# Turned transposes in the set-up of a state-space branch, and two idle products on TensorE

## The chip, the cores and the metric

The kernel runs on one core of a Trainium2 chip, as one launch. The metric is the time of the launch on the device in microseconds (us). The core's engines are TensorE (PE in the profile; its weight loads are the row PEld), VectorE (DVE), ScalarE (ACT), GpSimd (POOL) and SyncE (SP). Each works off its own queue of instructions in order and waits on semaphores for what the others make. SP's and POOL's queues also hold the instructions that start DMA transfers: one that waits holds up all behind it on that queue.

## What is computed

One layer of an encoder over 512 tokens of width 1024, with 256 fixed memory tokens, in fp32:

```
n = rms_norm(h);  proj = n @ w_in            # columns: xa 512, zu 1024, zv 1024, gate_a 1024, gate_b 1024
ya = s5_branch(xa)                           # two diagonal state-space scans (forward, backward), 32 groups of 16
     y = d*u + scan_fwd(u) + scan_bwd(u);  y = gelu(y);  ya = y * sigmoid(y @ w_glu)
yb = sgu_branch(zu, zv)                      # gating by 128x128 position matrices
h = h + (gate_a*(ya @ w_proj_a) + gate_b*(yb @ w_proj_b)) @ w_out
q = rms_norm(h) @ w_q;  k, v = memn @ w_k, memn @ w_v    # memn = rms_norm(mem); 4 heads of 256
h = h + softmax(q k^T / 16) v @ w_o
h = h + (silu(n @ w_gate) * (n @ w_up)) @ w_down;  out = rms_norm(h)
```

## The kernel before, in words

**Products.** Every fp32 operand is split into a high and a low half in a reduced format: ScalarE casts the high half (L85), VectorE subtracts it for the low one (L86). A product is three matmuls, high by high, high by low, low by high (`mm3`, L358). `feat` makes two banks of 128 channels x 512 tokens at a time (tiles `pf`), `tokm` makes banks of 128 tokens x 512 channels (`pt`). For w_proj_b, w_q and the feed-forward part the kernel multiplies 2x2 blocks with seven products instead of eight (`product`, L1110; 128x256 each), on sums of blocks that are made ahead. The intermediate banks of w_proj_b are `bx`, `bq`, and `qv` for a copy of a bank by ScalarE that later products go on adding to (`seed`, L1123). `gated` (L1173) multiplies a bank with a gate in `part`; the last one is `gated(1, 1, T0, minus(bq, u1))`, where `u1` lies in the tile `zf[0]`.

**Weights** come through a plan: three raw buffers filled by DMAs on SP's queue (L137, L224), split two blocks ahead of their use into three buffers of halves.

**The S5 branch as a side program.** `s5_program` is a Python generator: set-up, kernels of octets 0 and 1, inputs, scan, outputs, with the kernels of octets 2 and 3 between the outputs. The main program calls `tick(us)` after each block of products; a tick adds credit (0.8 of the block's time) and runs the generator until the credit is used up. `yield 1.1` costs 1.1 of it; `yield None` ends the tick and sets the credit to nothing. `later(n, fn)` puts a function off by n steps of 5.2 us.

- Set-up (L625 on): the input and output matrices are loaded as rows (`brow`, `crow`) and turned on TensorE, 8 transposes (L657) and 4 transposes (L664) to an auxiliary PSUM bank, each bank copied by ScalarE to `raw_b` (L658) or `raw_c` (L665).
- Kernels (`pk`, L814-817) are matrices of 8x8 steps within a chunk, stored to DRAM and loaded back. Inputs: `pw` transposes (L864), `pz` products (L871). The scan (L890-901) is a chain of small VectorE operations on `zh`, one step for each of 64 chunks.
- Outputs, for each octet of groups: four copies of states `ss` on ScalarE (L916, L917), 24 products pairwise `py` (L922 to L924), gelu to `y` (L929), and eight stores `yd` to DRAM (L932), by turns on SP and POOL.

**Merging.** `finish_side` runs the rest of the side program. Then four loads `ygt` (SP, L1222) bring the S5 outputs back in another layout; they are split to `yg` and multiplied by w_glu; the sigmoid (L1229), the product `glu` (L1231) and a split give `ya`, which goes through w_proj_a. The rows of gains `g_mem` and `g_x` are loaded on SP (L471); they use the two buffers of the tag "gain", one of which is `zf[0]`'s.

**Order.** The framework builds the program with a scheduler that simulates a timeline (`schedule_with_timeline_sim=True`) and chooses the order on every engine; `tc.keep_in_program_order` fixes single instructions (`in_order`), among them the loads of `g_mem` and `g_x` and the idle products. An idle product is a matmul of 128x512 to an auxiliary bank that nobody reads:

```python
    def idle_product(x, y):
        in_order(nc.tensor.matmul(aux("idle"), x[:, 0, 0:P], y[:, 4, :], start=True, stop=True))
```

There are two in the kernel already, at the second query product and in the feed-forward part. Auxiliary banks are three; the banks of the main products are five.

**Keys.** After w_out, `feat` makes the keys (`w_k`, four pairs of tiles of 128x256), then `tokm` the values (`w_v`), then follow the queries (`qx`, `qq`).

Of the kernel before, what the change touches and what calls it, by code (L numbers as in the profile page):

```python
# [9 lines left out]
F32 = mybir.dt.float32  # L10
# [7 lines left out]
P = 128  # L18
# [8 lines left out]
G = 32  # L27
C = 16
# [13 lines left out]
NO = 4  # L42
# [10 lines left out]
def hybrid_layer_kernel(  # L53
# [8 lines left out]
    nc = tc.nc  # L62
# [14 lines left out]
    def bank(name):  # L77
        return pm.tile([P, 512], F32, tag="mm", name=name)

    def aux(name, shape=(P, 512)):  # L80
        return pa.tile(list(shape), F32, tag="aux", name=name)
# [248 lines left out]
    def next_w(*key):  # L330
        i = used_w[0]
        used_w[0] += 1
        assert len(plan[i][0]) == len(key) and plan[i][0][1:] == key[1:] and plan[i][0][0] is key[0]
        for j in range(i, min(i + FAR + 1, len(plan))):
            begin(j, i)
            if j - 1 >= len(tiles) and j - 1 <= i + SPLITS:
                split_w(j - 1)
        for j in range(len(tiles), min(i + SPLITS + 1, len(plan))):
            split_w(j)
        tile_, tiles[i] = tiles[i], None  # L340
        return tile_
# [20 lines left out]
    def feat(w, c0, act, nk, evac, n=T, kpt=4, parts=1, ps=None, part=None):  # L362


        if part is not None:
            for kb in range(0, nk, kpt):
                feat_block(ps, (kb,) + next_w(w, kb, kpt, c0, 256), act, nk, kpt, part[0], not part[1])
                tick(2.6)
            if part[1]:
                for j in range(2):  # L370
                    evac(c0 // P + j, j, ps[j])
            return
        ps = ps or [bank("pf0"), bank("pf1")]
        ws = []
        for kb in range(0, nk, kpt):
            ws.append((kb,) + next_w(w, kb, kpt, c0, 256))
            if parts == 1:
                feat_block(ps, ws.pop(), act, nk, kpt, slice(0, n))
                tick(5.2 * n / T)
        for i in range(parts if parts > 1 else 0):  # L380
            for x in ws:
                feat_block(ps, x, act, nk, kpt, slice(i * n // parts, (i + 1) * n // parts))
            tick(5.2 * len(ws) / parts)
        for j in range(2):
            evac(c0 // P + j, j, ps[j][:, :n])

    def feat_block(ps, x, act, nk, kpt, tsl, fresh=True):

        kb, hi, lo = x
        for j in range(2):  # L390
            cs = slice(j * P, (j + 1) * P)
            for k in range(kpt):
                kk = kb + k
                mm3(ps[j][:, tsl], (hi[:, k, cs], lo[:, k, cs]), (act[0][:, kk, tsl], act[1][:, kk, tsl]),
                    kk == 0 and fresh, kk == nk - 1, not fresh)
# [47 lines left out]
    def later(n, fn):  # L443

        side["later"].append((side["now"] + n, fn))
# [7 lines left out]
    def tick(us=5.2):  # L453

        side["now"] += us / 5.2
        run_due()
        side["credit"] = min(side["credit"] + us * side["rate"], us)
        while side["credit"] > 0.0 and side["gen"] is not None:
            try:
                used = next(side["gen"])  # L460
            except StopIteration:
                side["gen"] = None
                return
            if used is None:
                side["credit"] = 0.0
                return
            side["credit"] -= used
# [8 lines left out]
    ident = cp.tile([P, P], F32, name="ident")  # L476
# [61 lines left out]
    def slot(tag, shape, dt, name, place=NEAR):  # L538
        n = math.prod(shape[1:])
        t = sp.tile([P, KD * T + ROOM[tag]], dt, tag=tag, name=name)[:, place[tag]:place[tag] + n]  # L540
        return t.rearrange("p (a b c) -> p a b c", a=shape[1], b=shape[2]) if len(shape) == 4 else (
            t.rearrange("p (a b) -> p a b", a=shape[1]))

    def token_slot(name, place=NEAR):
        return tuple(slot(tag, (P, KD, T), F32R, name, place) for tag in "BC")
# [3 lines left out]
    s5p = s5.enter_context(tc.tile_pool(name="s5", bufs=1))  # L549
# [70 lines left out]
    def s5_setup():  # L620
        A_ = nc.scalar
# [3 lines left out]
        def small():  # L625
            used[0] += 1
            return slab[:, used[0] - 1, :]
# [6 lines left out]
        for i, src in enumerate((s5_lam_re, s5_lam_im)):  # L634
            nc.sync.dma_start(lrows[:, i], src[0].rearrange("d g p -> g d p"))
            ps = aux("plam", (P, G))
# [11 lines left out]
        crow = s5p.tile([P, 2, C // 4, 2, 64], F32, tag="tt", name="crow")  # L648
# [2 lines left out]
                nc.sync.dma_start(crow[:, i, :, d, :], src[0, d].rearrange("g (a b) p -> (g a) b p", a=4))  # L651
        bb = s5p.tile([P, 2, G, C], F32, name="raw_b")
        rows = brow.rearrange("g d p c -> g (d p) c")
        for n in range(2):
            ps = aux("pbc", (P, C // 2, 2 * G))
            for k in range(C // 2):
                nc.tensor.transpose(ps[:, k, :], rows[:, :, 8 * n + k], ident[:2 * G, :2 * G])  # L657
            A_.copy(bb.rearrange("p i g c -> p c (i g)")[:, 8 * n:8 * n + 8, :], ps)  # L658
            yield None
        cc = s5p.tile([P, 2, G, C], F32, name="raw_c")  # L660
        for i in range(2):
            ps = aux("pbc", (P, C // 4, P))
            for k in range(C // 4):
                nc.tensor.transpose(ps[:, k, :], crow[:, i, k].rearrange("q d p -> q (d p)"), ident)  # L664
            A_.copy(cc[:, i].rearrange("p g (a b) -> p b (g a)", a=4), ps)  # L665
            yield 0.1
        br, bi, cr, ci = bb[:, 0], bb[:, 1], cc[:, 0], cc[:, 1]
        st["c"] = (cr, ci)

# [1 line left out]
        stp, a, rho, th, n, sn, hs, cs = (small() for _ in range(8))  # L671
# [103 lines left out]
    def lc(t, g):  # L775
        return t[:, g].rearrange("p a b -> p (a b)")
# [127 lines left out]
    def s5_outputs(o):  # L904
        gs = slice(o * GO, (o + 1) * GO)
        while ("oct", o) not in st:
            yield None
        e_re, e_im, tt = st["oct", o]
        zh, u = st["zh"], st["u"]
        ss = s5p.tile([P, 2, GO, NCH], F32, tag="wt", name="ss", bufs=2)  # L910
        ss = (ss[:, 0], ss[:, 1])
        for i, s in enumerate(ss):
            zv = zh[:, :, i, gs].rearrange("p n g -> p g n")
            nc.gpsimd.memset(s[lo_, :, 0:1], 0.0)
            nc.gpsimd.memset(s[hi_, :, NCH - 1:NCH], 0.0)
            nc.scalar.copy(s[lo_, :, 1:NCH], zv[lo_, :, 0:NCH - 1])  # L916
            nc.scalar.copy(s[hi_, :, 0:NCH - 1], zv[hi_, :, 0:NCH - 1][:, :, ::-1])  # L917

        def mix_():
            ps = aux("py", (P, GO, NCH))  # L920
            for g in range(GO):
                nc.tensor.matmul(ps[:, g, :], tt[:, g, :], u[:, o * GO + g, :], start=True, stop=False)  # L922
                nc.tensor.matmul(ps[:, g, :], lc(e_re, g), ss[0][:, g, :], start=False, stop=False)
                nc.tensor.matmul(ps[:, g, :], lc(e_im, g), ss[1][:, g, :], start=False, stop=True)  # L924
            later(1, lambda: emit(ps))

        def emit(ps):
            y = s5p.tile([P, GO, NCH], F32, tag="y", name="y")
            nc.scalar.activation(y, ps, AF.Gelu_apprx_tanh)  # L929
            ydo = yd[o].rearrange("(g c) l n -> l c g n", c=C)  # L930
            for l in range(Q):
                (nc.sync, nc.gpsimd)[l % 2].dma_start(ydo[l], y[C * l:C * l + C])  # L932

        later(0.5, mix_)
        yield 0.1

# [123 lines left out]
    for h in range(H):  # L1060
        ps = bank("psv")
# [7 lines left out]
    yb_hi = slot("E", (P, KD, T), F32R, "yb_hi", AWAY)  # L1069
    yb_lo = slot("D", (P, KD, T), F32R, "yb_lo", AWAY)  # L1070
# [43 lines left out]
    def idle_product(x, y):  # L1114

        in_order(nc.tensor.matmul(aux("idle"), x[:, 0, 0:P], y[:, 4, :], start=True, stop=True))

    def unit_bank(name):
        return bank(name).rearrange("p (j t) -> p j t", j=2)
# [45 lines left out]
    for q, ts in ((5, T1), (6, T0)):  # L1165
        for i in range(2):
            k = slice(2 * i, 2 * i + 2)
# [98 lines left out]
    hn_hi, hn_lo = token_slot("hn", AWAY)  # L1266
# [53 lines left out]
    def v_evac(half):  # L1320
        def f(t, ps):
            if not vts:
                vt = ap_.tile([P, 2, NM, D], F32R, tag="vt", name="vt", bufs=1)
                vts.extend((vt[:, 0], vt[:, 1]))
            vt_hi, vt_lo = vts
            cs = slice(half * 512, half * 512 + 512)
            split(vt_hi[:, t, cs], vt_lo[:, t, cs], ps)
        return f
# [20 lines left out]
    later(2, token_sums)  # L1349
    for c0 in range(0, D, 256):  # L1350
        feat(w_k, c0, mn, KD, k_evac, n=M)
    for half in range(2):
        tokm(w_v, half * 512, mn, KD, v_evac(half), ntok=NM)

# [132 lines left out]
    for t0 in (0, 2):  # L1487
        ps = {t: bank(f"pt{t - t0}") for t in (t0, t0 + 1)}
# [77 lines left out]
    ps = [bank("pf0"), bank("pf1")]  # L1566
# [67 lines left out]
    for i, u in enumerate(UNITS):  # L1634
        final = i == len(UNITS) - 1
        x, v = begun
        q = unit_bank("pq")
# [132 lines left out]
    for i in range(2):  # L1770
        p = aux("pcut", (P, 256))
# [37 lines left out]
```

## Time and profile before

| | |
|---|---|
| median of three runs | 892.44 us (892.33 to 893.95) |
| profiled execution | 893.12 us, span 891.3 us |
| mean granted TensorE clock | 0.997 |
| PE busy | 881.1 us, 99% of the span, 5744 records |
| DVE busy | 642.5 us, 72% |
| ACT busy | 487.4 us, 55% |
| POOL busy | 106.9 us, 12% |

The span runs from the first to the last instruction in the profile; the execution's own time is 1.8 us longer. Matmuls are pipelined: each record overlaps the next, so the pace of products is the distance of their starts, or the duration of a piece of the chain divided by its count. The chain is the sequence of work that ended last, followed back from the last instruction. A bracket at the end of a row tells how long the engine was idle before it and what released it. In a row of a stretch (start:end) stand its length, the busy time of PE, PEld, DVE, ACT and POOL with the number of instructions, the granted PE clock, the busy share of the DMA engines and GB/s.

### The profile page before, as it was taken

To read this page: it belongs to the slowest core of one execution; us is meant where nothing else is said; L and a number is where in the kernel's file an instruction comes from. 1 tells how busy PE (TensorE), PEld (TensorE's weight loads), DVE (VectorE), ACT (ScalarE), POOL (GpSimd) and SP (SyncE) were. 2 spreads that over 40 slices of the span, in tenths; PEclk is the share of its full clock that TensorE was granted. 3 is DMA by queue.
4 is the path that set the end of the run, shared out by engine and by line. 5 is a ranking of instruction groups with operands and counts; after the bars stand their busy time and mean duration, and the time that the engine had idled before them with its cause. 6 is when DMAs were issued, how large, how long until landed. Compare 5 with 4: busy or idle time off the path is not lost.

```text
span 891.3 us, 14796 instructions
## 1 busy us (share of the span) xinstructions
PE 881.1 (99%) x5744; PEld 788.0 (88%) x5744; DVE 642.5 (72%) x1048; ACT 487.4 (55%) x714; POOL 106.9 (12%) x165
## 2 busy tenths in 40 slices
PE   9999999999999999999999999999999999999996
PEld 6788888888889998889899978999999999988875
DVE  5697653889847368658856836676878777899875
ACT  5743994244396254347656534645555455655664
POOL 1005301111032111001001001101121111000010
PEclk9999999999999999999999999999999999999998
DMA  8667456978533789834579747627899999356672
GB/s 255 196 189 182 114 155 177 189 191 190 159 87 84 212 285 268 288 117 140 168 221 256 194 103 197 166 81 181 213 237 233 216 225 249 95 167 207 204 230 102
DMA packets 118408, 165.36 MB, mean 186 GB/s; under 512 B 11825, under 2 KB 84161, under 8 KB 118210
## 3 DMA queue, kind: packets, MB, share of 16 engines
q1 hardware_dynamic: 97474, 135.74, 47.9%
q0 software_dynamic: 20576, 28.15, 19.9%
q8 instruction: 45, 0.74, 0.3%
q10 hardware_dynamic: 288, 0.52, 0.2%
q14 instruction: 25, 0.20, 0.1%
HBM read 157.61 MB, written 46.63 MB: 229 GB/s over the span
## 4 chain that ended last, share of the span: by engine, by line
PE 97%; DMA 1%; SPq 1%; ACT 0%; DVE 0%; issue 0%; POOLq 0%; ACTq 0%
PE pf L358 26%; PE pt L358 17%; PE px L1110 12%; PE dx L358 6%; PE pq L1110 6%; PE dq L358 3%; PE pv L1110 3%; PE bx L1110 3%; PE qx L1110 2%; PE dv L358 2%; PE pz L871 2%; PE pk L814 2%; PE bq L1110 1%; PE qv L1110 1%; PE psc L358 1%; PE qq L1110 1%
## 5 line engine op out<-in xcount | busy, mean ns | idle before, releaser
L86 DVE TENSOR_TENSOR wlo<-wraw,whi 128x1024 fp32r<-128x1024 f32 (+1 forms) x145 | 172.2, 1189 | 101.2 <-ACT whi L85 101.0
L85 ACT CAST whi<-wraw 128x1024 fp32r<-128x1024 f32 (+1 forms) x145 | 148.6, 1026 | 152.2 <-PE pf L358 44.0
L358 PE MATMUL pf<-xn,whi 128*128 128x512 f32 x448 | 139.6, 391 | 0.0
L358 PEld LDWEIGHTS pf<-xn,whi 128*128 128x128 f32 x448 | 83.7, 188 | 17.0
L358 PE MATMUL pf<-xn,wlo 128*128 128x512 f32 x224 | 87.3, 390 | 0.0
L1110 PE MATMUL px<-fn,whi 128*128 128x256 f32 x480 | 83.4, 277 | 0.0
L1110 PEld LDWEIGHTS px<-fn,whi 128*128 128x128 f32 x480 | 72.7, 188 | 0.2
L85 ACT CAST whi<-b 128x1024 fp32r<-128x1024 f32 x40 | 42.2, 1055 | 50.4 <-PE px L1110 27.4
L86 DVE TENSOR_TENSOR wlo<-b,whi 128x1024 fp32r<-128x1024 f32 x40 | 48.9, 1223 | 27.0 <-ACT whi L85 27.0
L1110 PE MATMUL px<-fn,wlo 128*128 128x256 f32 x240 | 66.4, 277 | 0.0
L1110 PE MATMUL pq<-s,whi 128*128 128x256 f32 x320 | 55.0, 276 | 0.0
L358 PE MATMUL dx<-whi,s 128*128 128x512 f32 x170 | 53.4, 390 | 0.4 <-DVE h L1734 0.4
L85 ACT CAST whi<-t 128x1024 fp32r<-128x1024 f32 x30 | 31.6, 1054 | 35.6 <-PE pv L1110 12.4
L86 DVE TENSOR_TENSOR wlo<-t,whi 128x1024 fp32r<-128x1024 f32 x30 | 36.7, 1225 | 19.7 <-ACT whi L85 19.7
L358 PEld LDWEIGHTS pf<-xn,wlo 128*128 128x128 f32 x224 | 42.1, 188 | 8.7
L1110 PEld LDWEIGHTS pq<-s,whi 128*128 128x128 f32 x320 | 48.3, 188 | 0.0
L1110 PEld LDWEIGHTS px<-fn,wlo 128*128 128x128 f32 x240 | 45.1, 188 | 0.0
L358 PE MATMUL pt<-whi,xn 128*128 128x512 f32 x128 | 43.7, 412 | 0.7 <-ACT xn L85 0.7
L1110 PE MATMUL pq<-s,wlo 128*128 128x256 f32 x160 | 44.2, 276 | 0.0
L358 PEld LDWEIGHTS dx<-whi,s 128*128 128x128 f32 x170 | 31.8, 188 | 7.5 <-issue 0.8
L358 PE MATMUL dx<-wlo,s 128*128 128x512 f32 x85 | 33.0, 390 | 0.0
L275 POOL DMA_DIRECT2D dsum<-in_w_down_dram x12 | 13.3, 1105 | 162.4 <-DMA dsum<-in_w_down_dram 162.4
(453 smaller groups left out, 2296.8 us busy)
## 6 DMA issues: line engine op xcount, KB each, us to landing
wraw<-in_w_in_dram SPq DMA_DIRECT2D x36, 512.0 KB, 4.7
dsum<-in_w_down_dram SPq DMA_DIRECT2D x20, 512.0 KB, 5.4
wraw<-dsum SPq DMA_DIRECT2D x20, 512.0 KB, 4.1
b<-in_w_gate_dram SPq DMA_DIRECT2D x15, 512.0 KB, 5.4
b<-in_w_up_dram SPq DMA_DIRECT2D x15, 512.0 KB, 5.3
wraw<-in_w_down_dram SPq DMA_DIRECT2D x15, 512.0 KB, 4.4
dsum<-in_w_down_dram POOLq DMA_DIRECT2D x10, 512.0 KB, 8.1
dsum<-dsum POOLq DMA_DIRECT2D x10, 512.0 KB, 8.5
```

The costliest lines, as they stand in the source:

```text
L85: hi = nc.scalar.copy(dst_hi, src)
L86: lo = nc.vector.tensor_tensor(dst_lo, src, dst_hi.bitcast(F32), ALU.subtract)
L275: plan[j + step][1].append((0, lambda d=dst, x=more: nc.gpsimd.dma_start(d, x, accum_op=ALU.add)))
L358: m = nc.tensor.matmul(ps, a[x], b[y], start=start and i == 0, stop=stop and i == 2, skip_group_check=free)
L814: nc.tensor.matmul(ps[32 * j:32 * j + 32, q, :], bd[i][:, g].rearrange("p d c -> p (d c)"), lc(es[i], g), start=(i == 0), stop=False, tile ...
L871: nc.tensor.matmul(ps[:, g, :], wt[:, g, :], u[:, o * GO + g, :], start=True, stop=True)
L1110: nc.tensor.matmul(ps[:, j, :], a[x], b[y], start=start and j == k == i == 0, stop=k == 3 and i == 2, skip_group_check=True)
```

## The change

1. In the set-up the tile `raw_c` is allocated earlier, the generator stops once more before the transposes, and the groups of `brow` and `crow` take turns: brow 0, crow 0, brow 1, crow 1, with a `yield None` after each. Before, both groups of brow came first (`yield None` after each), then both of crow (`yield 0.1` after each).
2. In `s5_outputs`, an idle product of 512 columns follows the `py` products of the last octet.
3. In the keys' loop, an idle product follows the second pair of key tiles (c0 = 256).

Lines after the first edit keep their number up to L923; from the second on they are 2 higher, from the third on 4 higher.

```diff
--- before.py
+++ after.py
@@ -651,19 +651,19 @@
                 nc.sync.dma_start(crow[:, i, :, d, :], src[0, d].rearrange("g (a b) p -> (g a) b p", a=4))
         bb = s5p.tile([P, 2, G, C], F32, name="raw_b")
         rows = brow.rearrange("g d p c -> g (d p) c")
+        cc = s5p.tile([P, 2, G, C], F32, name="raw_c")
+        yield None
         for n in range(2):
             ps = aux("pbc", (P, C // 2, 2 * G))
             for k in range(C // 2):
                 nc.tensor.transpose(ps[:, k, :], rows[:, :, 8 * n + k], ident[:2 * G, :2 * G])
             A_.copy(bb.rearrange("p i g c -> p c (i g)")[:, 8 * n:8 * n + 8, :], ps)
             yield None
-        cc = s5p.tile([P, 2, G, C], F32, name="raw_c")
-        for i in range(2):
             ps = aux("pbc", (P, C // 4, P))
             for k in range(C // 4):
-                nc.tensor.transpose(ps[:, k, :], crow[:, i, k].rearrange("q d p -> q (d p)"), ident)
-            A_.copy(cc[:, i].rearrange("p g (a b) -> p b (g a)", a=4), ps)
-            yield 0.1
+                nc.tensor.transpose(ps[:, k, :], crow[:, n, k].rearrange("q d p -> q (d p)"), ident)
+            A_.copy(cc[:, n].rearrange("p g (a b) -> p b (g a)", a=4), ps)
+            yield None
         br, bi, cr, ci = bb[:, 0], bb[:, 1], cc[:, 0], cc[:, 1]
         st["c"] = (cr, ci)
 
@@ -922,6 +922,8 @@
                 nc.tensor.matmul(ps[:, g, :], tt[:, g, :], u[:, o * GO + g, :], start=True, stop=False)
                 nc.tensor.matmul(ps[:, g, :], lc(e_re, g), ss[0][:, g, :], start=False, stop=False)
                 nc.tensor.matmul(ps[:, g, :], lc(e_im, g), ss[1][:, g, :], start=False, stop=True)
+            if o == NO - 1:
+                idle_product(yb_hi, yb_lo)
             later(1, lambda: emit(ps))
 
         def emit(ps):
@@ -1349,6 +1351,8 @@
     later(2, token_sums)
     for c0 in range(0, D, 256):
         feat(w_k, c0, mn, KD, k_evac, n=M)
+        if c0 == 256:
+            idle_product(hn_hi, hn_lo)
     for half in range(2):
         tokm(w_v, half * 512, mn, KD, v_evac(half), ntok=NM)
```

## The prediction

> **What bounds the kernel now.** I read the engines' busy time first, then the shares of the chain of work that ended last.
>
> ```profile
> span 891.3 us, 14796 instructions
> PE 881.1 (99%) x5744; PEld 788.0 (88%) x5744; DVE 642.5 (72%) x1048; ACT 487.4 (55%) x714; POOL 106.9 (12%) x165
> PE 97%; DMA 1%; SPq 1%; ACT 0%; DVE 0%; issue 0%; POOLq 0%; ACTq 0%
> ```
>
> PE is busy for 99% of the span and holds 97% of the chain. So there is almost no PE wait to win: a change can gain only by shortening the products themselves, and it loses every microsecond that PE waits. The questions are what the products' cadence is, and whether the new order of the built program leaves PE without work. For both I went to the chain in order of time around each place that moves.
>
> ```profile
> 84.24 5.24 PE pt L358 x23
> 151.88 10.30 PE pf L358 x45
> 250.92 0.75 PE pf L358 x3
> 256.53 5.31 PE pf L358 x23
> 261.84 1.41 PE bx L1110 x12
> 315.19 2.83 PE bx L1110 x24
> 323.44 2.83 PE bq L1110 x24
> 326.26 23.84 PE pf L358 x105
> 419.18 10.96 PE pf L358 x93
> 430.13 22.40 PE pt L358 x96
> 452.53 2.74 PE qx L1110 x24
> 573.99 2.83 PE pv L1110 x24
> 577.05 13.05 PE pf L358 x115
> ```
>
> The columns are start, duration, what, count. Products of 512 columns run at two paces: 5.24/23 = 0.228 us and 22.40/96 = 0.233. Those of 256 columns too: 2.74/24 = 0.114 and 2.83/24 = 0.118. At 576.8 there is an idle product; 0.118 stands before it and 13.05/115 = 0.1135 behind it. An idle product of this kind can thus change the pace from slow to fast, by about 4%.
>
> **The change part by part.** The two idle products themselves: the row at 576.82 ends where the next begins, at 577.05, so each takes 0.23 us of PE: +0.5 together. What they can win is the slow stretches behind them: 55 products of 256 columns after the last py (7 bq, 24 bx, 24 bq), 54 left of w_k, 96 of w_v. At 0.004, 0.004 and 0.0055 us each that is 0.2 + 0.2 + 0.5 = 0.9; bounds 0 (no change of pace) and 0.9. I take -0.9, as the pair of rows around 577 is the same case.
>
> The transposes by turns: no instruction is added or removed by this, the eight and four transposes of a group and its copy are the same. But the setup is a generator that the main program steps forward, and a yield of None ends a step and sets its credit to nothing. The setup now stops five times where it stopped two times with None and two times with 0.1, so it comes about three steps later, and the scheduler then places all S5 work later. In the order of the built program, pw and pz stand in smaller groups: 24 breaks of the 512-column runs up to the first psv instead of 18. A break costs next to nothing (the 23 products above took 0.228 each, next to a pw group on one side and pz on the other): +0.2, bounds 0 and 0.4. The last pz group moves behind 29 more products. Before, 45 lay between it and psv (the row at 151.88); now 16. The scan of the states can begin only 29 x 10.30/45 = 6.6 us later.
>
> **A, the wait behind the scan.** These rows show ACT and VectorE where the scan ends.
>
> ```profile
> 244.30 0.23 DVE L901 TENSOR_TENSOR zh<-sa,sb 128x64 f32<-128x64 f32 x1
> 244.56 1.10 ACT L916 COPY ss<-zh 64x504 f32<-64x504 f32 x1 [0.88 <-DVE zh L901]
> 252.29 1.05 ACT L917 COPY ss<-zh 64x504 f32<-64x504 f32 x1
> 255.87 1.28 ACT L929 ACT_TABLE_LOAD   x1
> 263.48 0.60 ACT L1138 ACTIVATE part<-pf 128x512 f32<-128x512 f32 x1
> 264.11 2.18 ACT L85 CAST s<-zf 128x512 fp32r<-128x512 f32 x4
> 266.69 1.99 ACT L85 CAST whi<-wraw 128x1024 fp32r<-128x1024 f32 x2
> 268.57 0.58 ACT L1123 COPY qv<-bx 128x512 f32<-128x512 f32 x1
> ```
>
> The scan ended at 244.53 and so ends at 244.53 + 6.6 + 0.2 = 251.3. Two octets' ss copies (eight, 244.56 to 253.34, 8.8 us) bring ACT to 260.1. In the built order there stand, from there to the seed copy qv that the next products wait for: a sigmoid 0.6, four s casts 2.18, a sigmoid 0.6, a weight cast 1.0, a table load 1.28, y 0.6, four ss copies 4.4, two s casts 1.1, a weight cast 1.0, qv 0.58 = 13.3, to 273.4. PE's side: the first py octet lay at 250.7 to 250.92 and 251.67 to 256.53 = 5.1 us ahead of bx, and now stands behind the first bx. So bx starts at 261.84 - 5.1 + 0.2 = 256.9, and PE has 24 bx and 24 bq (48 x 0.116 = 5.6), py 5.1 and a product of pk before it needs qv: it gets there at about 267.9. PE waits 273.4 - 267.9 = 5.5 us. Bounds: 3, if ACT takes the casts while PE is still ahead (that is half), and 6.6, the scan's whole delay. I take +5.4, as the rows sum to it. The VectorE's own list to pk in that stretch (subtracts, e, dd) is shorter. **B:** at the second seed (v1), ACT has four ss copies 4.4, a weight cast 1.0 and the copy 0.58 = 6.0 us behind py of the second octet, PE only 34 bx and one pk, 34 x 0.116 + 0.2 = 4.1: +1.9, bounds 0 (ACT ran ahead) and 2.5.
>
> **C, the w_glu products wait for yg.** In the built order SyncE's queue now has g_mem and g_x ahead of the four ygt loads; before, both stood behind. g_x takes the buffer of zf[0], which the very last gated (zf<-bq, L1132, then part<-zf, L1173) still reads. So nothing of ygt is issued before the last bq product is done, and the next products on PE are pf<-yg, which need it.
>
> ```profile
> 320.72 0.69 DVE L1132 TENSOR_TENSOR u<-bq,u 128x512 f32<-128x512 f32 x1 [0.47 <-PE bq L1110]
> 321.44 0.69 DVE L1173 TENSOR_TENSOR part<-u,part 128x512 f32<-128x512 f32 x1
> 330.19 0.68 DVE L1173 TENSOR_TENSOR part<-zf,part 128x512 f32<-128x512 f32 x1
> 330.72 0.51 SPq L274 DMA_DIRECT2D qsum<-qsum  x1
> 331.33 0.53 SPq L471 DMA_DIRECT2D g_x<-in_xattn_norm_g_dram  x1
> 318.44 1.77 SPq L1222 DMA_DIRECT2D ygt<-yd  x4
> 311.57 0.60 ACT L929 ACTIVATE y<-py 128x512 f32<-128x512 f32 x1 [6.34 <-PE py L924]
> ygt<-yd SPq DMA_DIRECT2D x4, 256.0 KB, 4.1
> g_mem<-in_mem_norm_g_dram SPq DMA_DIRECT2D x1, 512.0 KB, 9.6
> 321.95 0.62 ACT L85 CAST yg_hi<-ygt 128x512 fp32r<-128x512 f32 x1 [0.37 <-DMA ygt<-yd]
> ```
>
> Call the end of the last bq E. A gated pair starts some 0.1 us after its bank (320.61 to 320.72) and ends 1.4 later (320.72 to 322.13): E + 1.5. From the end of part<-zf (330.87) to the start of g_x's issue are 0.46, most of it another load's issue (to 331.23), so I count 0.3; the issue takes 0.53: ygt's first issue is at E + 2.3. From issue to landing a ygt load took 4.1 in the median, and 318.44 to 321.95 = 3.5 the first one; half a megabyte of g_x is now just ahead of it, and g_mem of that size took 9.6. I take 4.7, a little over the median. The cast adds 0.62 and a tenth for the hand-over: E + 7.7. Bounds 6.5 (3.5) and 12.6 (9.6). Before, the loads were issued 7.8 us ahead of E (326.26 - 318.44) and the whole chain from y's start to the first cast's end (311.57 to 322.57, 11.0 us) was hidden behind the 14.7 us of bx and bq that follow the last py. Of these 125 products 55 are left (6.4 us), so even with the queue's order as before some 4.6 us of that chain would show. y and its stores start 6.4 us before E and are done when ygt is issued: they add nothing to C. The Trainium skill ("DMA: Bandwidth & Descriptors", section "Issuing engines are not separate DMA queues") says that DMAs started by different engines run on the same 16 DMA engines and interleave. By it the half megabyte of g_x would slow ygt whichever engine issued it; that agrees with taking more than the median, and no run here shows its size.
>
> **After the wait.** These rows show how PE starts after idling, at the beginning of the kernel.
>
> ```profile
> 10.23 0.63 PE L358 MATMUL pt<-wlo,xn 128*128 128x512 f32 x1
> 10.66 1.05 PE L358 MATMUL pt<-whi,xn 128*128 128x512 f32 x2
> 12.85 0.50 PE L358 MATMUL pt<-wlo,xn 128*128 128x512 f32 x1
> 13.65 0.40 PE L358 MATMUL pt<-wlo,xn 128*128 128x512 f32 x1
> 13.89 0.62 PE L358 MATMUL pt<-whi,xn 128*128 128x512 f32 x2
> ```
>
> From 10.23 to 10.66 one product takes 0.43 us, from 13.65 to 13.89 one takes 0.24: about seven at the start ran at twice the time. If a wait of 8 us brings that state back, it costs 7 x 0.2 = +1.4; bounds 0 and, if A's wait does it too, 2.8. I take 1.4. The Trainium skill ("TensorE: Matmul & The Clock Gate", "What's actually happening") says that the clock falls to half after one idle window of some 3.4 us and is whole again after about 3.4 us of work. By that both waits would be followed by it, and the sum would be about 1.4 higher. **D:** after w_glu come ACT's sigmoid, VectorE's glu and two halves of ya for each of four banks, before w_proj_a can go on; in the built order the four banks of w_glu are taken by turns and so end together, where before the first two ended early. I take +0.8, bounds 0 and 2 (one bank's glu, 1.15, and a cast).
>
> **The sum** is +0.5 - 0.9 + 0.2 + 5.4 + 1.9 + 7.7 + 1.4 + 0.8 = +17.0 against the profiled execution, which took 893.1 us (span 891.3 and 1.8 around it): 910.1. The median of the three runs, 892.4, is 0.7 lower, so I say 909.4. Low ends throughout: 0.5 - 0.9 + 0 + 3 + 0 + 6.5 = +9.1, so 901.5 against the median. High ends: 0.5 + 0.4 + 6.6 + 2.5 + 12.6 + 2.8 + 2 = +27.4, which needs every mishap at once.
>
> **The rivals.** *ygt lands as late as g_mem did.* If the loads of ygt queue behind the gain's half megabyte as a whole, C is 12.6 and the time 909.4 + 4.9 = 914.3. For it: the row with 9.6; against it: ygt's own 4.1 was taken in a stretch of 1.01 DMA share as well (below).
>
> ```profile
> 320.00:327.00 7.00, 7.00 (x58) 6.85 (x57) 6.28 (x9) 4.39 (x6) 0.00 (x0) 1.00 1.01 339
> ```
>
> *Only the wait for yg counts.* If ACT works the ss copies off earlier than I place them (the scan's delay is taken up by an ACT that is 55% busy), A and B vanish: 909.4 - 7.3 = 902.1. For it speaks ACT's idle time; against it, that the eight ss copies and all the rest in between are one queue in a fixed order.
>
> *The change shortens the kernel or leaves it.* The mechanism: in the run itself the scan and the last gated come early enough, because the order in the program is only an order, and PE's products hide ygt's chain; what remains is the pace. Then +0.5 - 0.9 = -0.4, so 892.0, so within 0.2%; it would take slow stretches elsewhere to turn fast as well (the 93 products at 419.18 cost 10.96 where 93 x 0.1135 = 10.56) to come lower by more. It decides if ygt could be issued 5.4 us (4.7 and the cast) ahead of E, and it can't while g_x waits for the last gated. I hold it for little.
>
> *The idle products don't change the pace at all* (at 455.3 one stands between two stretches of the same pace, 2.74 and 2.73 for 24): +0.9, inside the first case.
>
> **How the numbers follow.** Forecast with its bounds (904 to 913) 0.66; ygt as late as g_mem 0.13; only yg 0.15; no slower 0.06. The range takes in the first three with the high bound of the pauses: 900 to 916. Slower by over 0.2% (1.8 us, about what a measurement of this kernel can tell from no change) 0.94; within 0.2% 0.03; faster 0.03, from the last case in halves.
>
> **What would show it.** In the profile of the changed kernel: PE idle ahead of the first pf<-yg with ygt's landing as its releaser, 6.5 to 12.6 us; ygt issued behind part<-zf; some products at 0.43 us after that; idle on PE ahead of qv with the copy at L1125 as releaser, 3 to 6.6 us; 0.1135 and 0.228 us per product behind the idle of w_k. The forecast is wrong if ygt is issued before the last bq ends, or if PE never waits for the scan's copies.

## The result and the profile after

The changed kernel took 914.78 us (median of five runs, 914.27 to 917.19) against 892.71 for the kernel before (892.33 to 893.95): a ratio of 1.0251, 95% interval 1.0235 to 1.0267. It is 22 us slower; 909.4 was forecast, with a range of 900 to 916. The profiled execution has a span of 912.5 us, 21.2 more than before.

First the page of the changed kernel (span and engines), then its view of what TensorE waited for: engine, operation, releaser, us in total, times, longest.

```profile
span 912.5 us, 14798 instructions
PE 882.0 (97%) x5746; PEld 789.1 (86%) x5746; DVE 643.8 (71%) x1048; ACT 485.2 (53%) x712; POOL 106.6 (12%) x165
```

```profile
PE pf L358 <- ACT yg_hi L85: 9.6, 1, 9.6
PE pk L814 <- DVE e L795: 4.4, 1, 4.4
PE qv L1112 <- ACT qv L1125: 3.3, 2, 1.8
```

No engine does much more work: PE is 0.9 us busier over a span that is 21.2 longer, VectorE 1.3. The three lines are new and make 17.3 us. (The view's next line, 1.9 us, lies at the kernel's start; at the first psv, the position products of the gating branch at 162 us, the two kernels are 0.2 us apart.) Where the time goes is seen from the same products in the chain of both kernels. These pieces are of the changed kernel.

```profile
332.17 2.73 PE bq L1112 x24
334.93 0.70 DVE zf L1134
335.65 0.70 DVE part L1175
336.37 0.35 SPq L471
337.80 5.89 DMA ygt<-yd
343.86 0.63 ACT yg_hi L85
344.52 5.68 PE pf L358 x15
...
445.28 0.23 PE idle L1118
445.51 6.13 PE pf L358 x54
451.64 21.97 PE pt L358 x96
473.61 2.75 PE qx L1112 x24
```

The last bq ends at 334.90; it ended at 326.26 before, so 8.6 us are lost by then. The first yg product starts at 344.52 against 326.26: 18.3. The values (pt) start at 451.64 against 430.13: 21.5. The first query product starts at 473.61 against 452.53: 21.1, and the end of the span keeps that. In between, the first ya product gives the step behind yg; its rows in the two timelines:

```profile
337.02 0.62 PE L358 MATMUL pf<-ya_hi,whi 128*128 128x512 f32 x2
```

```profile
357.53 0.61 PE L358 MATMUL pf<-ya_hi,whi 128*128 128x512 f32 x2
```

That is 20.5. So 8.6 us lie before the end of bq, 9.7 in the wait for yg, 2.2 in w_glu, 1.0 in w_proj_a and what follows it, and 0.4 are won in the values.

**The granted clock.** The view by stretches, of the changed kernel: start and end, length, busy time of PE, PEld, DVE, ACT, POOL (instructions), granted PE clock, DMA share, GB/s.

```profile
273.90:277.20 3.30, 3.30 (x15) 3.30 (x16) 2.98 (x3) 0.91 (x1) 0.00 (x0) 0.50 0.37 118
277.20:281.00 3.80, 3.80 (x36) 3.80 (x35) 2.54 (x3) 1.06 (x1) 0.00 (x0) 1.00 0.55 178
298.00:302.00 4.00, 4.00 (x35) 4.00 (x36) 4.00 (x5) 2.92 (x4) 2.10 (x4) 1.00 0.51 71
334.90:344.50 9.60, 0.00 (x0) 0.00 (x0) 2.52 (x3) 1.57 (x2) 1.34 (x2) 0.69 1.01 333
344.50:348.90 4.40, 4.38 (x10) 3.47 (x11) 2.25 (x4) 2.04 (x4) 0.00 (x0) 0.51 1.13 299
348.90:352.00 3.10, 3.10 (x15) 2.58 (x14) 0.52 (x1) 1.09 (x1) 0.00 (x0) 1.00 1.10 411
```

Behind the first wait, 15 products of 256 columns take 3.3 us, 0.22 each instead of 0.113, at a granted clock of 0.50. Behind the wait for yg, ten products of 512 columns take 4.4, 0.44 instead of 0.227, at 0.51. Each time the clock is whole again some 3.3 to 4.4 us later. Behind the second qv wait (ends at 297.97) it stays at 1.00.

**Why the first wait is there.** Rows of VectorE and ScalarE in the changed kernel:

```profile
250.97 0.23 DVE L901 TENSOR_TENSOR zh<-sa,sb 128x64 f32<-128x64 f32 x1
262.20 2.50 DVE L86 TENSOR_TENSOR s<-zf,s 128x512 fp32r<-128x512 f32 x4 [8.72 <-ACT s L85]
270.53 1.22 DVE L795 TENSOR_TENSOR e<-e,etmp 128x1024 f32<-128x1024 f32 x1
```

```profile
252.13 1.13 ACT L916 COPY ss<-zh 64x504 f32<-64x504 f32 x1
261.55 2.18 ACT L85 CAST s<-zf 128x512 fp32r<-128x512 f32 x4
273.26 0.58 ACT L1125 COPY qv<-bx 128x512 f32<-128x512 f32 x1
```

The scan ends at 251.2, 6.7 us later than before. Then ScalarE copies the states of two octets, to 260.9; VectorE stands idle for 8.7 us behind an s cast that is queued after them, and only then comes to `e`, which pk needs. PE waits for `e` to 271.8 and then for the seed copy qv to 273.9. ScalarE works without a pause from 251.2 to 273.8, and its copy ends last: had `e` come sooner, PE would have had to wait for qv all the same.

### The profile page after: what moved, and what is told of

It reads as the page before. It is cut to its first block, busy times and chain, and to the rows that moved or that the text cites. A ratio compares the mean times of both kernels' runs of the same rounds, so it can differ in the third digit from the quotient of the medians.

```text
span 912.5 us, 14798 instructions
## 1 busy us (share of the span) xinstructions
PE 882.0 (97%) x5746; PEld 789.1 (86%) x5746; DVE 643.8 (71%) x1048; ACT 485.2 (53%) x712; POOL 106.6 (12%) x165
## 4 chain that ended last, share of the span: by engine, by line
PE 67%; ACT 1%; DMA 1%; issue 1%; DVE 1%; SPq 0%; POOLq 0%; ACTq 0%; DVEq 0%
PE pt L358 12%; PE px L1112 12%; PE pf L358 9%; PE dx L358 6%; PE pq L1112 6%; PE dq L358 3%; PE pv L1112 3%; PE qx L1112 2%; PE bx L1112 2%; PE dv L358 2%; PE qv L1112 1%; PE psc L358 1%; PE qq L1112 1%; PE po L358 1%; PE ptr L520 1%; PE bq L1112 1%
```

## The experiments

Each run is compared with runs of the kernel before on the same chip.

**1. The set-up alone.** The changed kernel without its two idle products; the order on the other engines is then the changed kernel's, instruction for instruction.

```diff
-            if o == NO - 1:
-                idle_product(yb_hi, yb_lo)
...
-        if c0 == 256:
-            idle_product(hn_hi, hn_lo)
```

> The changed kernel without its two idle products: only the set-up's transposes by turns, with five ends of a step. Theory: the set-up alone makes the loss, and the idle products only add 0.23 us each and win about 0.65 us behind the one among the keys, so the time is 914.5 to 915.5 us. Rival: the idle product behind the last py delays the path to yg; then the time is 913 or less.

916.27 us against 894.13: ratio 1.0259 (1.0230 to 1.0288), which overlaps the changed kernel's; the time lies above the 914.5 to 915.5 expected. The set-up makes the loss; an interval this wide can't place the idle products' few tenths. Two pieces of this run's chain say more:

```profile
301.85 4.63 PE qv L1110 x24
337.56 2.84 PE bq L1110 x24
```

The first stands behind the second qv wait, 1.86 us here and 1.85 in the changed kernel, where the same 24 products took 3.00. In run 1 fifteen of them start 0.21 us apart, in the changed kernel none. With the same order on every engine up to there, 1.6 us were lost or not. The second is the last bq: without the idle product behind the last py it runs at 0.118, with it (2.73 for 24) at 0.1135. From the first product behind the last py to the end of bq run 1 needs 6.55 us for 55 products, the changed kernel 6.26.

**2. The idle products alone.** The kernel before with both; on every engine but PE the order is that of before, and on PE only the two are added.

```diff
+            if o == NO - 1:
+                idle_product(yb_hi, yb_lo)
...
+        if c0 == 256:
+            idle_product(hn_hi, hn_lo)
```

> The kernel before with the two idle products and the old set-up. Theory: the idle products turn the slow pace behind them to the fast one: 124 products of 256 columns behind the last py (0.0045 us each, 0.55), 54 of the keys (0.24) and the 96 of the values in part (0.4), for 0.47 us of their own: 0.7 us faster, 891.7 to 892.2. Rival: the pace is not theirs to change: 0.5 us slower, 893.2.

892.63 us against 894.13: ratio 0.9991 (0.9974 to 1.0007). The times can't tell it from no change; the chain can:

```profile
322.39 2.72 PE bq L1112 x24
422.82 6.13 PE pf L358 x54
428.94 21.97 PE pt L358 x96
```

Before, 24 of those bx or bq took 2.83, and 96 pt took 22.40. Behind the last py 125 products now take 14.18 us and took 14.77; behind the idle product of the keys 54 run at 0.1135, and the values at 0.229, between the two paces (their starts lie 0.226, 0.229 and 0.232 apart, by turns). That is 0.59 + 0.24 + 0.43 won and some 0.5 spent: about 0.8 us in sum, near the 0.7 expected. The span of this profile is only 0.9 shorter, and 0.7 of that is there before the first idle product; counted from the first psv, 0.9 are won to the first query product and 0.7 lost again in the last 125 products (`dx`, of the feed-forward part), 0.5 of it in a wait for a weight block that the kernel before does not have. Run 11, the same program, wins the same 0.9 and loses 0.6 of it behind the first query product, in other places.

**3. The gains behind ygt.** The line that loads `g_mem` and `g_x` is moved behind w_proj_a; ScalarE's and GpSimd's orders do not change.

```diff
-    g_mem, g_x = gain(mem_norm_g, "g_mem", True), gain(xattn_norm_g[0], "g_x", True)
...
     for c0 in range(0, D, 256):
         feat(w_proj_a, c0, (ya_hi, ya_lo), 4, pa_evac)
+    g_mem, g_x = gain(mem_norm_g, "g_mem", True), gain(xattn_norm_g[0], "g_x", True)
```

> The changed kernel, but the two loads of gains stand behind the ygt loads on SyncE's queue (their line is moved behind w_proj_a). Theory: ygt then waits for the stores of yd alone (issued to 330.83 in the profile of the changed kernel, landed by about 333) and lands some 4 us later, at 337; the wait of PE falls from 9.7 to about 3 us, and the slow start behind it shrinks: 905 to 908 us. Rival: the wait is for the stores and the transfers' own time, not for the queue: 912 or more.

914.58 us against 894.13: ratio 1.0235 (1.0219 to 1.0250). The expectation of 905 to 908 fell. PE's wait for yg, then SP's row in the timeline ahead of ygt, then the time to landing in the view of ygt:

```profile
PE pf L358 <- ACT yg_hi L85: 6.5, 1, 6.5
```

```profile
336.74 0.40 SPq L137 DMA_DIRECT2D wraw<-in_w_proj_a_dram  x1
```

```profile
DMA to landing us min/median/max: 5.3/5.5/5.7
```

With the gains gone from the queue, another load stands ahead of ygt: one of w_proj_a, which waits for a raw buffer. ygt is issued at 337.62 and so as late as in the changed kernel (337.15), but it lands in 5.3 to 5.7 us. So the wait shrank by 3.1 us only. Half of that was lost earlier: here the second qv wait, of the same length, was followed by a clock of 0.53 (run 3's stretch behind it):

```profile
298.70:302.30 3.60, 3.60 (x17) 3.60 (x18) 3.60 (x5) 1.86 (x3) 2.10 (x4) 0.53 0.50 68
```

Run 1 has this loss without the moved loads, so it is not their doing. In this profile it hides some 1.6 us of what the shorter wait was worth. Another 0.9 went in w_glu, which took 13.9 us to the first ya product and 13.0 in the changed kernel.

**4. The gains ahead of ygt in the kernel before.** The set-up is the old one; only the loads' place differs, with ygt's pinned behind them.

```diff
+    g_mem, g_x = gain(mem_norm_g, "g_mem", True), gain(xattn_norm_g[0], "g_x", True)
     for m in range(4):
-        nc.sync.dma_start(ygt[:, m, :], yd[m].rearrange("p l n -> p (l n)"))
+        in_order(nc.sync.dma_start(ygt[:, m, :], yd[m].rearrange("p l n -> p (l n)")))
```

> The kernel before, with the two loads of gains ahead of the ygt loads on SyncE's queue and nothing else changed up to there. Theory: this alone makes PE wait about 9.7 us for yg and start slowly behind it (10 products at 0.44 us, 2 us): 903 to 906 us. Rival: the wait in the changed kernel came from the late scan and the short cover behind the last py; here the 14.7 us of cover are left, and the time is 896 or less.

906.20 us against 894.13: ratio 1.0144 (1.0128 to 1.0159), 12 us, just above the 903 to 906 expected. PE's wait, SP's rows, ygt's time to landing, and the stretch behind the wait:

```profile
PE pf L358 <- ACT yg_hi L85: 11.4, 1, 11.4
```

```profile
326.90 0.35 SPq L471 DMA_DIRECT2D g_x<-in_xattn_norm_g_dram  x1
327.30 2.86 SPq L1223 DMA_DIRECT2D ygt<-yd  x4
```

```profile
DMA to landing us min/median/max: 8.0/8.2/8.5
```

```profile
336.80:340.70 3.90, 3.90 (x9) 3.12 (x10) 2.47 (x4) 2.88 (x4) 0.00 (x0) 0.51 1.06 236
```

The stores of yd are long done here, and 14.7 us of products cover them. g_x, which waits for the last gated, is enough for a wait of 11.4 and a half-speed stretch.

**5. The stops alone.** The transposes in their old sequence, with the three added ends of a step.

```diff
+        yield None
         for n in range(2):
             ps = aux("pbc", (P, C // 2, 2 * G))
...
             A_.copy(cc[:, i].rearrange("p g (a b) -> p b (g a)", a=4), ps)
-            yield 0.1
+            yield None
```

> The kernel before with the three added ends of a step alone: one before the transposes, and None in place of 0.1 behind the two groups of crow; the transposes keep their old sequence, and there are no idle products. Theory: it is the later set-up, not the turning, that moves the scan and puts the loads of gains ahead of ygt; the loss is of the changed kernel's kind, 905 to 917 us. Rival: the turning makes the loss; then 896 or less.

919.65 us against 893.82: ratio 1.0268 (1.0246 to 1.0289). The stops alone make a loss as large as the changed kernel's, even somewhat larger than expected: PE waits 14.2 us for yg and 8.5 for qv. ygt lands in 5.3 to 5.9 us here, with g_x issued 6.7 us ahead of it and not just ahead. PE's waits, what SP waited for ahead of ygt, and a row of GpSimd:

```profile
PE pf L358 <- ACT yg_hi L85: 14.2, 1, 14.2
PE qv L1111 <- ACT qv L1124: 8.5, 2, 6.9
```

```profile
SPq L1223 <- DMA yd<-y: 4.0, 1, 4.0
335.40 1.20 POOL L275 DMA_DIRECT2D qsum<-in_w_q_dram  x1 [12.49 <-DMA qsum<-qsum]
```

The wait for yg has another last cause here than in the changed kernel. The gains stand ahead of ygt too, and g_x is issued at 337.76; but what ygt waits for last are the stores of yd. GpSimd issues its four behind a blocked load of its own, from 336.06 to 338.72, and they land at 344.0; ygt is issued at 344.46, 8.2 us behind the last bq (336.28) and not 2.3. The first wait for qv, 6.9 us, is the one that the prediction called A, with ScalarE's seed copy as releaser.

**6. The turns with the old stops.** Against the changed kernel, which has a stop more ahead of the groups and None behind the brow groups:

```diff
-        yield None
         for n in range(2):
...
             A_.copy(bb.rearrange("p i g c -> p c (i g)")[:, 8 * n:8 * n + 8, :], ps)
-            yield None
+            yield 0.1
...
-            if o == NO - 1:
-                idle_product(yb_hi, yb_lo)
...
-        if c0 == 256:
-            idle_product(hn_hi, hn_lo)
```

> The transposes by turns, with as many ends of a step as before (none ahead of them, 0.1 behind each brow group, None behind each crow group), and no idle products. Theory: with the set-up no later, the gains stay behind ygt and no wait arises: 892 to 895 us. Rival: the turning itself moves the scan or crowds ScalarE: 900 or more.

898.59 us against 893.82: ratio 1.0049 (1.0034 to 1.0064). Neither expectation held. The large waits are gone and the gains stand behind ygt, but this version is 4.8 us slower than the kernel before. Its profile shows no wait above 1.8 us, and that one lies at the kernel's start. Its span is 5.6 us longer: 1.0 up to the first psv, 1.8 from there to the last bq (a wait of 0.8 for an s cast among them), 1.2 in w_glu (1.1 of it a wait for ya) and 1.6 behind. Why they arise is left open.

**8. The same with the two idle products.**

```diff
+            if o == NO - 1:
+                idle_product(yb_hi, yb_lo)
...
+        if c0 == 256:
+            idle_product(hn_hi, hn_lo)
```

> The turns with as many ends of a step as before, and the two idle products. Theory: the two idle products win 0.7 us here as they did in the old order: 0.7 us below the run without them, 891.5 to 894. Rival: in this order the pace behind the last py is fast already, and they cost 0.2 to 0.5.

895.69 us against 893.82: ratio 1.0020 (1.0004 to 1.0036), 2.9 below run 6, where 0.7 was expected; with medians of 8 and 10 runs that vary by 4 us, the size is not settled. Of run 6's losses this profile has only the one between the first psv and the last bq (1.6 us). So this much goes with the turning in both runs, and what else the turning costs is not shown.

**7. The wait for yg filled** with 38 idle products.

```diff
+    for _ in range(38):
+        idle_product(yb_hi, yb_lo)
     yg_hi = mgp.tile([P, 4, T], F32R, name="yg_hi")
```

> The changed kernel with 38 more idle products of 512 columns between the last bq and the first pf<-yg, some 8.6 us in the wait of 9.7. Theory: they keep TensorE busy, so the half-speed start behind the wait (10 products at 0.44 us in the changed kernel) falls away, and the time is 912.5 to 914 us; yg still comes one block per 1.5 us, so not all 2.1 are won. Rival: the slow start is the wait for the later blocks of yg, and the products still take 0.44: 914.5 to 916.

914.24 us against 893.82: ratio 1.0220 (1.0201 to 1.0239). yg arrives when it did, but the clock stays whole:

```profile
336.00:344.00 8.00, 7.44 (x33) 5.82 (x31) 1.62 (x2) 0.17 (x2) 1.34 (x2) 1.00 0.93 321
344.50:348.90 4.40, 4.40 (x19) 3.63 (x20) 2.66 (x4) 2.99 (x4) 0.00 (x0) 1.00 1.14 280
```

In the same 4.4 us in which the changed kernel did ten products, nineteen ran. The slow products are therefore made by PE's idling and not by the data. Of the 2.1 us, 0.7 are left at the first ya product (356.80 against 357.53 in the changed kernel): PE now waits 1.1 us for later blocks of ygt, and 0.9 for ya. The loss against the kernel before is 20.4 us in place of 22.1; the time lies between the two expectations.

**9. ygt on GpSimd's queue.**

```diff
-        nc.sync.dma_start(ygt[:, m, :], yd[m].rearrange("p l n -> p (l n)"))
+        nc.gpsimd.dma_start(ygt[:, m, :], yd[m].rearrange("p l n -> p (l n)"))
```

> The changed kernel with the four ygt loads issued by GpSimd in place of SyncE, so that nothing but the stores of yd stands ahead of them; SyncE's queue keeps its order. Theory: the wait for yg is one of SyncE's queue; ygt is issued at about 333 on the changed kernel's clock in place of 337.15 and lands before g_x is under way, PE waits 3 to 5 us in place of 9.7, and the time is 907 to 911 us. Rival: the transfers themselves are slow in this stretch whoever issues them, and the time stays at 913 to 916.

925.79 us against 893.67: ratio 1.0353 (1.0335 to 1.0370), a loss some 10 us larger than the changed kernel's, and not what either theory had. GpSimd's rows, and ygt's time to landing:

```profile
341.67 1.20 POOL L275 DMA_DIRECT2D qsum<-in_w_q_dram  x1 [7.44 <-DMA qsum<-qsum]
...
342.98 2.22 POOL L1224 DMA_DIRECT2D ygt<-yd  x4
```

```profile
DMA to landing us min/median/max: 10.3/10.8/12.3
```

GpSimd's queue held a blocked transfer of its own: an accumulating load that waits for one of SyncE's. ygt was issued 5.8 us later than in the changed kernel and also took longer. The run doesn't answer the question it was made for.

**10. The first wait filled** with 18 idle products to a main bank, and **12.** with 28 of them.

```diff
     b_product(bq, 0, 5, True)
+    fill = bank("idle")
+    for _ in range(18):
+        in_order(nc.tensor.matmul(fill, yb_hi[:, 0, 0:P], yb_lo[:, 4, :], start=True, stop=True))
     b_product(bv, 0, 2)
```

> The changed kernel with 18 idle products of 512 columns (4.1 us) just ahead of the pk product that waits 4.4 us behind the scan. Theory: the 15 products of 256 columns behind that wait ran at 0.223 us because PE had idled; with the wait filled they run at 0.113, 1.6 us less, and the time is 912.5 to 914 us. Rival: they run slowly for another reason (their operands), nothing is won, and the time is 914.5 to 916.

905.30 us against 893.67: ratio 1.0128 (1.0108 to 1.0147), far faster than expected. The fill also moved the scheduler's choice: ygt now stands ahead of the gains and is issued at 330.05, so PE's wait for yg is 0.5 us. At the end of bq this kernel is as late as the changed one (335.1 against 334.9); all that it gains, it gains behind that point. What the run was made for it didn't answer: pk waits only 0.3 us, but qv does for 1.9, until 274.2 as in the changed kernel (273.9), and 17 slow products follow 1.4 us behind that. Two stretches:

```profile
274.00:275.60 1.60, 1.39 (x12) 1.39 (x13) 1.60 (x2) 1.14 (x2) 0.00 (x0) 1.00 0.00 0
275.60:279.20 3.60, 3.60 (x20) 3.60 (x19) 3.57 (x4) 0.90 (x1) 0.00 (x0) 0.53 0.67 201
```

```diff
-    for _ in range(18):
+    for _ in range(28):
```

> As the run with 18 idle products ahead of pk, but with 28 of them (6.3 us), so that both waits behind the scan (4.4 for pk and 2.2 for qv) are filled. Theory: a short idle of PE is enough to halve the pace of the products, but only some 1.5 us later and for about 3.5 us; with no idle left, none of the 24 qv and bx products behind it takes over 0.12 us (17 took 0.208 there with 18 idle products), and PE is 1.6 us earlier at the next py: a time of 903 to 905 us. Rival: the slow products come from something else than the idle; 17 of them at 0.2 us stay, and the time is 905.5 or more.

903.85 us against 894.17: ratio 1.0113 (1.0091 to 1.0135), within the 903 to 905 expected. With the waits ahead of qv filled, the clock is 1.00 in both stretches, and the qv products there take 0.118:

```profile
274.00:275.60 1.60, 1.60 (x15) 1.60 (x14) 1.60 (x2) 0.87 (x1) 0.00 (x0) 1.00 0.04 10
275.60:279.20 3.60, 1.77 (x25) 1.61 (x24) 3.57 (x4) 0.00 (x0) 0.00 (x0) 1.00 0.77 218
```

The order has moved again, though: only 14 qv products stand here, and an idle of 1.8 us is left in the second stretch, where pk waits for `e` from 276.3 to 278.1. No half speed follows that one (1.00 to 282). So this run shows fast products behind a filled wait, but not that every short idle costs time.

**11. The idle products alone, in more rounds** (the edit of run 2).

> The kernel before with the two idle products and the old set-up once more, in more rounds, as the version that may beat both kernels. Theory: 0.7 us faster, a ratio of 0.9992, too little for a measurement of this kernel to tell from no change unless the interval closes in. Rival: as the first medians had it, 1.5 us, a ratio of 0.998.

892.95 us against 893.67: ratio 0.9998 (0.9984 to 1.0011). No version here beats the kernel before by more than a measurement can tell.

## Why the prediction was right, and where its sizes were off

The direction, the range and the mechanism held; the forecast was 5.4 us short. The result lies above the 904 to 913 that the forecast itself was given, and inside the range by the part that was added for the pauses and for a late ygt. Term by term, in the changed kernel's profile:

| term | forecast | measured |
|---|---|---|
| scan ends | 251.3 | 251.2 |
| A, first waits | 5.4 | about 6.3 (4.4 for pk, 1.9 with hand-over for qv) |
| half clock behind A | 0 (to 1.4 more) | 1.6 (15 x 0.109) |
| B, second seed | 1.9 | 1.9 |
| C, yg | 7.7 | 9.7 |
| half clock behind C | 1.4 | 2.1 (10 x 0.21) |
| D | 0.8 | 1.0, in w_proj_a |
| idle products, own time | 0.5 | 0.5 |
| breaks | 0.2 | not seen by themselves |
| pace behind the idle product in w_k | -0.7 | -0.65 |
| pace behind the last py | -0.2 | -0.3, against run 1 |
| pace elsewhere | 0 | about -1, what is left of the sum |

- **A** came where it was put, but its first releaser was not ScalarE's seed copy. "The VectorE's own list to pk in that stretch (subtracts, e, dd) is shorter" was wrong: VectorE had to wait for ScalarE's s cast first, and its list then ended behind PE. Two engines stood one behind the other, and the prediction had them side by side. This did not set the length of A: ScalarE's copy still ended last, at 273.8 where 273.4 was forecast, and in run 10, with the wait for `e` filled, PE waits for it all the same.
- **The half clock behind A** was a bound and not a term. By the rule of the Trainium skill that the prediction cited ("TensorE: Matmul & The Clock Gate", "What's actually happening"), both waits should have been followed by it. The trace agrees: 0.50 and 0.51, each for 3.3 to 4.4 us. Adding it would have brought the forecast to 910.8. Idles shorter than the window that the rule names (some 3.4 us) don't keep to it: waits of 1.84 to 1.94 us were followed by half speed in runs 1, 3 and 10, and waits of 1.83 and 1.85 were not in run 12 and the changed kernel. Here the measurement decides.
- **Luck in B.** That the second wait cost 1.9 and not 3.5 was luck: run 1, in the same order, lost 1.6 us behind it. With that the changed kernel's time would have been some 916.4, just past the range.
- **C** was under-sized in one number, the landing: 4.7 was taken, and the first block took 6.5 (337.15 to the landing at 343.7). The issue at E + 2.3 was right (337.15 against 334.90). The other three loads, which the view has, took 7.3 to 9.3 us, where 3.4 to 5.3 was normal:

```profile
DMA to landing us min/median/max: 7.3/8.3/9.3
```

  Run 4 has g_x just ahead and 8.0 to 8.5; run 3 has it not and 5.3 to 5.7; run 5 has it far ahead and 5.3 to 5.9. That the half megabyte just ahead costs some 3 us fits these, though no run changed it alone. By the Trainium skill ("DMA: Bandwidth & Descriptors", "Issuing engines are not separate DMA queues") loads interleave on the same DMA engines whichever engine starts them. The trace of run 9, the only one with ygt on another engine's queue, agrees as far as one run can: ygt took 10.3 to 12.3 there, with g_x under way beside it to 345.7. ygt didn't become as late as g_mem did before (9.6 to landing); that rival had the total nearly right, 914.3, with one cause for what were three.
- **The rival with only the wait for yg** falls: 8.6 us were lost before it. **The other side** falls as it was put, on g_x's wait for the last gated; run 4 shows that wait alone.
- **The idle products** do change the pace, as forecast, though the one in w_k left the values at 0.229, between the two paces. The one behind the last py won its 0.2 to 0.3 in the changed kernel too: the products ahead of the last py are fast there already, and in run 1 as well, but in run 1 those behind it are slow again. The fast stretches ahead of it, which the kernel before doesn't have, came with the new order.
- That **the set-up's added stops** and not the transposes move the work held (runs 5 and 6), but the turning was taken at +0.2 with its breaks, and runs 6 and 8, which have it without the later set-up, lose 1.8 and 1.6 us between the first psv and the last bq. In the changed kernel this can't be told from A.

The two halves nearly add up: run 4, with the wait for yg alone, loses 12 us, and run 10, with the late scan and no long wait for yg, loses 11.6; the changed kernel, with both, loses 22. Pieces that were not separated: A is shown by rows, and its slow stretch by rows and by runs 10 and 12, but no run removed the late scan alone.

## What to carry to other kernels

When a scheduler places the work, read the built order on every queue: a load that needs a late buffer, put ahead of one that is needed now, can put that one's whole chain on the critical engine, here 12 us for two moved loads (run 4). Moving the held-up load to another queue (run 9), or taking the blocker out (run 3), helps only if nothing else there waits. To the length of a wait on TensorE the half-speed stretch that may follow it has to be added, and an experiment that adds instructions may move the rest, so the new order has to be read there too.

## What the runs showed of the hardware

A wait of TensorE of 1.8 to 1.9 us was followed by half speed in some runs and not in others: in the changed kernel the clock stayed at 1.00 behind the second qv wait, in run 3 it fell to 0.53 behind the same wait, and in run 1, with the same order on every engine up to there, the slow products began 0.6 us after work had begun again; in run 10 they began 1.4 us after it, and behind run 12's idle of 1.8 us the clock stayed at 1.00. The stretch was 3.3 to 3.6 us long at 256 columns. So a short idle can cost 1.6 us or nothing; what decides between them is not shown. The loss is set by PE's activity: with idle products in the long gap it was gone (run 7), and so it was behind the filled waits of run 12.

One idle product of 512 columns turned a slow pace of 256-column products (0.118) into a fast one (0.1133) at three places: in the kernel before at 576.8 us, and behind the last py and in w_k wherever a profile with it stands against one without (run 2 against before, run 8 against run 6, the changed kernel against run 1). That pace went on over 54 to 125 products; behind the 54, products of 512 columns ran at 0.229, between 0.2267 and 0.2333.
